# Indexer key, rope key and indexer weights in one half block, multiplied in float32, with rotary tables of half the width

## The chip, the cores and the metric

The kernel runs on one core of one Trainium2 chip, in one launch. The metric is device time in microseconds (us). The kernel before took 1176.38 us as the median of three runs (1176.0, 1177.55 and 1176.38 us). The engines are PE (TensorE, which multiplies matrices), DVE (VectorE), ACT (ScalarE), POOL (GpSimd) and SP (SyncE, which issues the transfers). Each runs its instructions in a fixed order and waits for the others by semaphores.

## The reference, cut to what matters

One decoder layer on 256 tokens of width 1024. A combined projection gives the inputs of two attention branches. Branch A selects 64 keys for each query by an indexer, and its rotary encoding covers all 64 dimensions of a head. Branch B is a latent attention with a rotary key of 32 dimensions. The gates merge the two, and 32 experts with a top-4 router follow.

```python
SPLITS = (A_WIDTH, A_WIDTH, A_WIDTH, IDX_HEADS * IDX_DIM, IDX_DIM, IDX_HEADS,
          Q_LORA, KV_LORA, QK_ROPE, 2 * D_MODEL)
def rope(x, positions):
    half = x.shape[-1] // 2
    inv_freq = ROPE_THETA ** (-jnp.arange(half, dtype=jnp.float32) / half)
    ...
    cos, sin = jnp.cos(ang).astype(x.dtype), jnp.sin(ang).astype(x.dtype)
    x1, x2 = x[..., :half], x[..., half:]
    return jnp.concatenate([x1 * cos - x2 * sin, x1 * sin + x2 * cos], axis=-1)
# the indexer of branch A, in a block of 128 queries
rel = jax.nn.relu(jnp.einsum('bthd,bsd->bths', qib, k_idx).astype(jnp.float32) * idx_scale)
score = jnp.einsum('bths,bth->bts', rel, wb.astype(jnp.float32) * w_scale)
...
_, sel = lax.top_k(score, k_sel)
```

Three of the narrow pieces of the projection matter here: the indexer key (`k_idx`, 64 columns), the indexer weights (`wb`, 8 columns) and the rope key (32 columns). Together they are 104 columns.

## The kernel before, in words

**The input projection.** The weights of the projection are packed on the host into blocks of 1 MB (`w_pre`), each of 128 partitions by 2048 numbers, and each block has two halves of 8 x 128 columns. A half gives 128 rows of a transposed result. The product is formed in three fp32r multiplications (L152 to L154): the weight is split into a high and a low part (`wh`, written by ACT at L143, and `wl`, the difference, written at L144 by DVE, or by POOL where the running number of the part stands in the list `POOL`), and the input likewise (`xh` at L148, `xl` at L149). So a half block is 24 matmuls of 256 columns: xh with wh, xl with wh, xh with wl for each of 8 slices. Up to three pairs of `wh` and `wl` are in use at a time.

**Block 0.** Its first half holds the indexer key twice (64 columns, repeated to fill 128), its second half the rope key twice and the indexer weights. Both halves land in one PSUM bank. `keys_first` copies the second result to SBUF (`kr_in`), and the two are rotated separately: `indexer_key` to `kim`, `rope_key` to `kr` and `kbm`.

**The rotary tables.** `rotary_tables` (L264 to L285) reduces the angles of two kinds of rotation on DVE, both side by side in tiles of 512 columns, and takes four sines of 256 columns on ACT. `tr_` serves branch A and the indexer, `trb` branch B. A rotation (`rope`, L204 to L208) is a shuffle of the source within groups of 32 partitions and a multiplication by the cosine on DVE, a multiplication by the signed sine on POOL, and an addition. The source may be a PSUM bank: the bank is free once the shuffle and the first multiplication have read it.

**PSUM.** The projection uses the tiles called `bank`, of which there are two. A third half block group can start on PE only after the readers of the first are done.

**What sets the order.** The list `ORDER` names the pieces of the head of the kernel in sequence (`k0` the keys, `tab` the tables, `ki` and `kr` the two rotations, `qi` the indexer queries, `lat` the latents, `ix` the indexer scores and so on). A scheduler then places the instructions of each engine by estimated durations, so that a change in one piece can move others. At L342 DVE forms the indexer scores, at L348 POOL masks them, at L352 and L353 DVE selects, eight at a time. At L375 DVE writes the low part of a latent, the last reader of that latent's bank.

**After the head.** From about 225 us the experts run, in pairs (L1021 and L1062 on PE). Their weights arrive as 1 MB transfers into a ring of slots. A slot is filled again as soon as PE has used it, and in the head the same ring carries the weights of the projection.

Of the kernel before, what the change touches and what calls it, by code (L numbers as in the profile page):

```python
# [52 lines left out]
POOL = "1 4 5 10 14 15 17 18 19 21 22 29 36 38 40 41 43"  # L53
# [4 lines left out]
def decoder_layer(ctx: ExitStack, tc: tile.TileContext, A, dbg=None):  # L58
# [59 lines left out]
    def load(i, k, n=2048):  # L118

        if i == 0:  # L120
            t = w0
        else:
            t = slot()
            sy.dma_start(t[:, :n], A["w_pre"][i][:, :n])
        return t[:, :n].rearrange("p (k c) -> p k c", k=k)
# [58 lines left out]
    for _ in range(20):  # L184
        te.matmul(idle[:, :P], ones, ones, start=True, stop=True)
# [54 lines left out]
    kr_in = work.tile([P, 1, T], F32, name="kr_in", tag="sq")  # L240
# [18 lines left out]
    def keys_first():
        for a in range(2):  # L260
            ps = half_proj(0, a)
        se.copy(kr_in, ps[:, 1:2])
        held["ki"] = ps

    def rotary_tables():
        pos = tmp1[:, 1]
        ve.tensor_copy(pos, pos_i)
        ang = tmp1[:, 2:4]
        ve.tensor_scalar(ang[:, 0], pos, cc[:, 0:1], None, op0=OP.mult)
        ve.tensor_scalar(ang[:, 1], pos, cc[:, 1:2], None, op0=OP.mult)  # L270
        rn = tmp2[:, 0:2]
# [4 lines left out]
        rc = tmp2[:, 2:4]  # L276
        ve.tensor_scalar(rn, ang, HALF_PI, -2 * math.pi, op0=OP.is_gt, op1=OP.mult)
        ve.scalar_tensor_tensor(rc, ang, HALF_PI, rn, op0=OP.add, op1=OP.add)

        for i, (src, j) in enumerate(((rc, 0), (ang, 0), (rc, 1), (ang, 1))):  # L280
            d = tr_[:, i] if i < 2 else trb[:, i - 2, 0]
            ve.tensor_scalar(d, src[:, j], PI_IN, -PI_IN, op0=OP.min, op1=OP.max)
            se.activation(d, d, AF.Sin)
            if i % 2:
                ve.tensor_scalar(d, d, cc[:, 2:3], None, op0=OP.mult)  # L285

    def indexer_key():
        rope(held["ki"][:, 0:1], 1, tab_a(1), [(kim, (slice(0, P), slice(0, 1)))])

    def rope_key():  # L290

        kr = work.tile([P, T], F32, name="kr", tag="sq")
        rope(kr_in, 1, [trb[:, i, 0:1] for i in range(2)],
             [(kr[:, None, :], (slice(0, P), slice(0, 1)))])
        for c in range(2):
            hs = slice(64 - 64 * c, 96 - 64 * c)
            se.copy(kbv[hs, :, c], kr[hs, None, :].to_broadcast([32, 4, T]))
        wiT = work.tile([64, T], F32, name="wiT", tag="sq")
# [298 lines left out]
    def router_tables():  # L597
# [6 lines left out]
        ge.tensor_scalar(lnv, lnv, cc[:96, 4:5], None, op0=OP.mult)  # L604
# [647 lines left out]
def _layout(inputs):  # L1252
# [13 lines left out]
    c[:, 0] = theta ** (-(p % 16 + 16 * (p // 32 % 2)).astype(np.float32) / np.float32(32))
    c[:, 1] = theta ** (-(p % 16).astype(np.float32) / np.float32(16))
    c[:, 2] = np.where(p % 32 < 16, -1.0, 1.0)
    c[:, 3] = p % 4 >= 2
    c[:, 4] = np.where(p // 8 % 4 == 1, np.float32(ALPHA), 1)  # L1270
# [17 lines left out]
```

## Time and profile before

| what | us |
|---|---|
| median of three runs | 1176.38 |
| the profiled execution | 1175.76 |
| its span, first to last instruction | 1174.1 |
| PE busy, over the span | 1089.6 (93%) |
| DVE busy | 333.3 (28%) |
| ACT busy | 221.8 (19%) |
| POOL busy | 136.3 (12%) |

The mean granted TensorE clock is 0.995 of full speed. The averages hide three stages. Up to about 225 us the projection, the attention and the router run, and all engines take part. From there to about 1105 us the experts run with the transfers at some 420 GB/s, and the last 69 us finish without new weights. The profiled execution is 0.62 us shorter than the median; the sums of this text are made against the profiled execution.

### The profile page before, as it was taken

To read this page: it belongs to the slowest core of one execution; us is meant where nothing else is said; L and a number is where in the kernel's file an instruction comes from. 1 tells how busy PE (TensorE), PEld (TensorE's weight loads), DVE (VectorE), ACT (ScalarE), POOL (GpSimd) and SP (SyncE) were. 2 spreads that over 40 slices of the span, in tenths; PEclk is the share of its full clock that TensorE was granted. 3 is DMA by queue.
4 is the path that set the end of the run, shared out by engine and by line. 5 is a ranking of instruction groups with operands and counts; after the bars stand their busy time and mean duration, and the time that the engine had idled before them with its cause. 6 is when DMAs were issued, how large, how long until landed. Compare 5 with 4: busy or idle time off the path is not lost.

```text
span 1174.1 us, 14174 instructions
## 1 busy us (share of the span) xinstructions
PE 1089.6 (93%) x5807; PEld 579.6 (49%) x5808; DVE 333.3 (28%) x702; ACT 221.8 (19%) x427; POOL 136.3 (12%) x127
## 2 busy tenths in 40 slices
PE   7999999999999999999999999999999999898985
PEld 7988889744343443434444444344444444343431
DVE  7887636713122111111111111111111111111113
ACT  4557734321011010101010101010101010101011
POOL 5574563200000100000001000000000000000001
PEclk9999999999999999999999999999999999999998
DMA  8433659799999999999999999999999999999993
GB/s 326 181 109 144 249 199 377 297 409 388 421 420 419 421 403 420 420 421 420 420 421 420 420 421 420 420 421 420 420 421 420 420 420 420 421 420 420 421 420 131
DMA packets 64239, 439.74 MB, mean 375 GB/s; under 512 B 8437, under 2 KB 8682, under 8 KB 11690
## 3 DMA queue, kind: packets, MB, share of 16 engines
q1 hardware_dynamic: 64170, 438.79, 91.3%
q8 instruction: 47, 0.77, 0.3%
q14 instruction: 22, 0.18, 0.0%
HBM read 437.71 MB, written 1.05 MB: 374 GB/s over the span
## 4 chain that ended last, share of the span: by engine, by line
DMA 55%; PE 28%; DVE 2%; ACT 1%; issue 0%; SPq 0%; DVEq 0%; ACTq 0%
DMA w<-w_up 36%; DMA w<-w_down 19%; PE pair L1021 13%; PE bank L1062 5%; PE misc L776 1%; PE pair L1062 1%; PE misc L977 1%; PE misc L154 1%; PE misc L152 1%; PE misc L153 1%; PE pair L152 1%; PE pair L154 1%; PE pair L153 1%; PE misc L910 0%; DMA braw<-b_down 0%; PE pair L790 0%
## 5 line engine op out<-in xcount | busy, mean ns | idle before, releaser
L1021 PE MATMUL pair<-w,xg 128*64 128x512 f32 x2032 | 490.0, 597 | 47.4 <-DMA w<-w_up 47.3
L1021 PEld LDWEIGHTS pair<-w,xg 128*64 128x64 f32 x2032 | 181.9, 136 | 314.7 <-issue 183.5
L1062 PE MATMUL bank<-w,y 128*64 128x512 f32 x960 | 213.2, 596 | 1.8
L1062 PEld LDWEIGHTS bank<-w,y 128*64 128x64 f32 x960 | 70.1, 137 | 127.5 <-issue 115.2
L889 DVE TENSOR_TENSOR acc<-acc,misc 128x512 f32<-128x512 f32 x60 | 38.7, 684 | 175.7 <-PE misc L977 175.6
L152 PE MATMUL bank<-xh,wh 128*128 128x256 f32 x256 | 73.9, 289 | 4.1 <-DVE rm L205 2.7
L899 DVE TENSOR_SCALAR y<-pair 128x512 f32<-128x512 f32 x32 | 22.0, 687 | 194.1 <-ACT y L892 194.1
L154 PE MATMUL bank<-xh,wl 128*128 128x256 f32 x256 | 72.9, 285 | 2.9 <-DVE wl L144 2.9
L153 PE MATMUL bank<-xl,wh 128*128 128x256 f32 x256 | 72.2, 282 | 1.3 <-DVE xl L149 1.3
L989 ACT CAST pgT<-bank 128x256 fp32r<-128x256 f32 x16 | 6.0, 373 | 340.3 <-PE bank L987 340.3
L776 PEld LDWEIGHTS misc<-pm,h 128*128 128x128 f32 x512 | 59.8, 192 | 13.3 <-issue 12.5
L178 POOL TENSOR_TENSOR rstd<-rstd,mhalf 128x1 f32<-128x1 f32 x4 | 2.6, 662 | 546.9 <-DVE rstd L684 546.9
L776 PE MATMUL misc<-pm,h 128*128 128x128 f32 x512 | 64.1, 278 | 0.0
L970 DVE SCALAR_TENSOR_TENSOR yp<-bank,gsl,yp 128x512 fp32r<-128x512 f32 x30 | 21.1, 745 | 148.2 <-ACT yp L968 148.2
L892 ACT ACTIVATE y<-pair 128x512 f32<-128x512 f32 x32 | 19.0, 597 | 192.8 <-PE pair L1021 192.8
L968 ACT ACTIVATE yp<-bank,gsl 128x512 fp32r<-128x512 f32 x30 | 19.0, 684 | 178.3 <-PE bank L1062 178.3
L152 PEld LDWEIGHTS bank<-xh,wh 128*128 128x128 f32 x256 | 48.8, 190 | 6.2 <-issue 3.0
L154 PEld LDWEIGHTS bank<-xh,wl 128*128 128x128 f32 x256 | 48.8, 191 | 4.0 <-DVE wl L144 3.8
L143 ACT CAST wh<-w 128x1024 fp32r<-128x1024 f32 (+1 forms) x42 | 42.7, 1024 | 41.9 <-PE bank L153 25.8
L153 PEld LDWEIGHTS bank<-xl,wh 128*128 128x128 f32 x256 | 48.9, 191 | 1.6 <-DVE xl L149 1.5
L768 DVE TENSOR_SCALAR xg<-misc,lnT 128x128 f32<-128x128 f32 x64 | 22.1, 404 | 92.5 <-PE misc L776 85.7
L144 DVE TENSOR_TENSOR wl<-w,wh 128x1024 fp32r<-128x1024 f32 (+1 forms) x26 | 40.4, 1554 | 16.1 <-ACT wh L143 16.1
(357 smaller groups left out, 1045.1 us busy)
## 6 DMA issues: line engine op xcount, KB each, us to landing
w<-w_up SPq DMA_DIRECT2D x254, 1024.0 KB, 19.8
w<-w_down SPq DMA_DIRECT2D x127, 1024.0 KB, 19.8
w<-w_pre SPq DMA_DIRECT2D x27, 1024.0 KB, 5.0
w<-w_pre SPq DMA_DIRECT2D x3, 512.0 KB, 7.3
w<-w_pre SPq DMA_DIRECT2D x2, 768.0 KB, 12.7
w<-xT SPq DMA_DIRECT2D x4, 256.0 KB, 6.4
xr<-x SPq DMA_DIRECT2D x2, 512.0 KB, 4.5
acc<-w_up SPq DMA_DIRECT2D x1, 1024.0 KB, 6.8
```

What stands on the lines that cost most here:

```text
L143: se.copy(hi, w[:, a])
L144: (ge if flip[0] in aside else ve).tensor_sub(lo, w[:, a], hi.bitcast(F32))
L152: te.matmul(out, lhs[0], rhs[0], start=start, stop=False)
L153: te.matmul(out, lhs[0], rhs[1], start=False, stop=False)
L154: te.matmul(out, lhs[1], rhs[0], start=False, stop=stop)
L768: ve.tensor_scalar(dst, src, lnT[:, k:k + 1], lnT[:, 8 + k:9 + k], op0=OP.mult, op1=OP.add)
L776: te.matmul(pt[:, k4], h[:, b, k * P:(k + 1) * P], pm[:, b].rearrange("p e s -> p (e s)"), start=(b == 0), stop=(b == NT - 1))
L889: ve.tensor_add(acc[:, b, half(c)], acc[:, b, half(c)], ps)
L899: ve.tensor_scalar(li, up[c][:, 1], LIMIT + 1.0, 1.0 - LIMIT, op0=OP.min, op1=OP.max)
L970: ve.scalar_tensor_tensor(y[:, 1, half(c)], dn[c], gs, y[:, 0, half(c)].bitcast(F32), op0=OP.mult, op1=OP.subtract)
L1021: te.matmul(up[c % 2][64 * i:64 * i + 64, c // 2], xg[k // 4][:, k % 4, 64 * i:64 * i + 64], ws[i][:, 512 * c:512 * c + 512], start=False, ...
L1062: te.matmul(dn[c][64 * i:64 * i + 64, :], aT[:, 2 * a + j, 64 * i:64 * i + 64], ws[i][:, D * j + 512 * c:D * j + 512 * c + 512], start=Fal ...
```

## The change

The 104 columns of indexer key, rope key and indexer weights now stand in one half block: key in rows 0 to 63, rope key in 64 to 95, weights in 96 to 103 of one result. It is multiplied in one pass of float32 (`mm8` on the unsplit input `xt` and weight), without `wh` and `wl`. Block 0 is loaded only in its first half. One rotation serves both keys, with a table (`tab`) of 256 columns a function in which rows 0 to 63 hold the angles of branch A and rows 64 to 127 those of branch B. ACT copies the halves of `tab` to where the wider tables were (`tr_`, `trb`), and copies the second half of `kim`. The constants shrink by a column, and the warm-up has 12 matmuls in place of 20. The list `POOL` is the same list of parts with all numbers two lower and without the first entry, because the two parts of block 0 are gone.

```diff
-POOL = "1 4 5 10 14 15 17 18 19 21 22 29 36 38 40 41 43"
+POOL = "2 3 8 12 13 15 16 17 19 20 27 34 36 38 39 41"
...
-    sy.dma_start(w0[:, D:], A["w_pre"][0][:, D:])
...
-    for _ in range(20):
+    for _ in range(12):
         te.matmul(idle[:, :P], ones, ones, start=True, stop=True)
...
     def keys_first():
-        for a in range(2):
-            ps = half_proj(0, a)
-        se.copy(kr_in, ps[:, 1:2])
-        held["ki"] = ps
+
+        ps = held["ki"] = bank()[:, None, :T]
+        w = w0[:, :D].rearrange("p (k c) -> p k c", k=KD)
+        mm8(ps[:, 0], lambda k: w[:, k], lambda k: xt[:, k])
...
-        for c in (C1, C2, C3):
+        for c in (C1, C2):
             ve.scalar_tensor_tensor(ang, rn, -c, ang, op0=OP.mult, op1=OP.add)
...
+        ve.scalar_tensor_tensor(tab[:, 1], rn, -C3, ang, op0=OP.mult, op1=OP.add)
+        ve.tensor_scalar(rn, tab[:, 1], HALF_PI, -2 * math.pi, op0=OP.is_gt, op1=OP.mult)
+        ve.scalar_tensor_tensor(tab[:, 0], tab[:, 1], HALF_PI, rn, op0=OP.add, op1=OP.add)
+
+        ve.tensor_scalar(tab, tab, PI_IN, -PI_IN, op0=OP.min, op1=OP.max)
+        se.activation(tab, tab, AF.Sin)
+        ve.tensor_scalar(tab[:, 1], tab[:, 1], cc[:, 1:2], None, op0=OP.mult)
 
     def indexer_key():
-        rope(held["ki"][:, 0:1], 1, tab_a(1), [(kim, (slice(0, P), slice(0, 1)))])
+        ps = held["ki"]
+        kr = held["kr"] = work.tile([P, 1, T], F32, name="kr", tag="sq")
+        rope(ps, 1, [tab[:, i, None] for i in range(2)],
+             [(kim[0:64], (slice(0, 64), slice(0, 1))), (kr[64:96], (slice(64, 96), slice(0, 1)))])
+        se.copy(kim[64:P], kim[0:64])
+        for c in range(2):
+            se.copy(tr_[64 * c:64 * c + 64], tab[0:64])
 
     def rope_key():
...
-        ve.tensor_scalar(wiT[32:40], kr_in[32:40, 0], 8 ** -0.5, None, op0=OP.mult)
+        se.activation(wiT[32:40], held["ki"][96:104, 0], AF.Copy, scale=8 ** -0.5)
...
-        ge.tensor_copy(trb[:, :, 1], trb[:, :, 0])
-        for i in range(2):
-            for c in range(2):
+        for c in range(2):
+            se.copy(trb[64 - 64 * c:P - 64 * c, :, c], tab[64:P])
+            for i in range(2):
                 ge.memset(trb[64 * c:64 * c + 64, i, c], 1.0 - i)
...
-    w8[:, :, 32:40] = wi[:, :, OWI:OWI + 8]
-    for i in (0, 64):
-        w8[:, :, i:i + ROPE] = wi[:, :, OKR:OKR + ROPE]
-    blocks = [flat(wi[:, :, 2 * [OKI + d for d in mixed]], w8)]
+    w8[:, :, :104] = wi[:, :, [OKI + d for d in mixed] + r(OKR, ROPE) + r(OWI, 8)]
+    blocks = [flat(w8)]
```

In the changed kernel the line numbers are lower: L143 and L144 become L139 and L140, L148 becomes L144, L152 to L154 become L148 to L150, L204 to L208 become L200 to L204, L342 becomes L334, L348 L340, L361 L353 and L375 L367.

First, ACT from its first cast on. Before, the table functions are the four at L283, and `kr_in` is the copy of the second key:

```order
L143 CAST wh<-w 128x1024 x3
L262 COPY kr_in<-bank 128x256
L143 CAST wh<-w 128x1024
L283 ACTIVATE tr__158<-tr__158 128x256
L283 ACTIVATE trb<-trb 128x256
L283 ACTIVATE tr__158<-tr__158 128x256
L143 CAST wh<-w 128x1024
L283 ACTIVATE trb<-trb 128x256
L143 CAST wh<-w 128x1024 x3
L297 COPY kbm<-kr 32x4x256 x2
```

The same place now, where L274 is the one sine, L284 and L298 the copies of its halves, and L289 takes the indexer weights out of the bank of the keys:

```order
L139 CAST wh<-w 128x1024 x3
L274 ACTIVATE tab<-tab 128x512
L284 COPY tr__149<-tab 64x512 x2
L298 COPY trb<-tab 64x2x256 x2
L139 CAST wh<-w 128x1024
L289 ACTIVATE wiT<-bank 8x256
L139 CAST wh<-w 128x1024
L291 COPY kbm<-kr 32x4x256 x2
L282 COPY kim<-kim 64x256
```

The last reader of the bank of the keys on ACT was the copy to `kr_in`, ahead of the tables; now it is L289, behind the sine, four copies and a cast.

Second, PE where the third latent (L152 on `bank_479` before, L148 on `bank_411` now) begins. Before, a whole latent on the bank `bank_407` stands ahead of it:

```order
L154 MATMUL bank_407<-xh_102,wl_409 128x256
L361 MATMUL misc_371<-ones_109,sq_403 128x1 x2
L226 MATMUL pair_682<-kim_153,rot_470 128x128
L152 MATMUL bank_479<-xh_102,wh_480 128x256
L153 MATMUL bank_479<-xl_103,wh_480 128x256
```

And now, with `bank_339` the second latent and `bank_272` the second pair of indexer queries, whose place in PSUM `bank_411` takes over:

```order
L150 MATMUL bank_339<-xh_101,wl_341 128x256
L150 MATMUL bank_272<-xh_101,wl_375 128x256
L148 MATMUL bank_272<-xh_101,wh_374 128x256
L149 MATMUL bank_272<-xl_102,wh_374 128x256
L150 MATMUL bank_272<-xh_101,wl_375 128x256
L148 MATMUL bank_272<-xh_101,wh_374 128x256
L149 MATMUL bank_272<-xl_102,wh_374 128x256
L150 MATMUL bank_272<-xh_101,wl_375 128x256
L353 MATMUL misc_303<-ones_108,sq_368 128x1 x2
L148 MATMUL bank_411<-xh_101,wh_412 128x256
```

The last seven matmuls of the indexer queries have moved behind the second latent, to just ahead of the third.

Third, POOL where the scores of the first 256 columns are masked. Before:

```order
L348 AFFINE_SELECT sc<-sc 128x128
L206 TENSOR_TENSOR rxs<-rxs,trb 128x512
L208 TENSOR_TENSOR rot<-rm,rxs 128x512
L348 AFFINE_SELECT sc<-sc 128x256
L144 TENSOR_TENSOR wl<-w,wh 128x1024 x2
L206 TENSOR_TENSOR rxs<-rxs,trb 128x512
```

And now:

```order
L340 AFFINE_SELECT sc<-sc 128x128
L202 TENSOR_TENSOR rxs<-rxs,trb 128x512
L204 TENSOR_TENSOR rot<-rm,rxs 128x512
L140 TENSOR_TENSOR wl<-w,wh 128x1024
L340 AFFINE_SELECT sc<-sc 128x256
L140 TENSOR_TENSOR wl<-w,wh 128x1024
```

One of the two low parts has moved ahead of the mask of 256 columns.

## Rows read from the trace of the kernel before

**Rows 1.** Page, part 2: GB/s moved in each of the 40 slices.

```profile
GB/s 326 181 109 144 249 199 377 297 409 388 421 420 419 421 403 420 420 421 420 420 421 420 420 421 420 420 421 420 420 421 420 420 420 420 421 420 420 421 420 131
```

**Rows 2.** Windows: span, busy of PE, PEld, DVE, ACT, POOL, clock, DMA share, GB/s.

```profile
25.00:50.00 25.00, 24.92 (x195) 23.44 (x196) 19.60 (x39) 14.17 (x21) 13.32 (x14) 0.93 0.57 225
50.00:60.00 10.00, 8.99 (x74) 8.63 (x74) 9.72 (x30) 4.23 (x7) 8.35 (x6) 1.00 0.32 116
205.00:220.00 15.00, 15.00 (x99) 13.63 (x98) 11.47 (x14) 6.62 (x9) 2.76 (x3) 1.00 0.62 226
463.00:1105.00 642.00, 593.37 (x2786) 267.08 (x2782) 106.27 (x214) 59.59 (x121) 4.73 (x6) 1.00 1.01 420
```

**Rows 3.** Chain of work that ended last: start, duration, what.

```profile
235.22 1.90 PE misc L776 x16
...
463.35 19.83 DMA w<-w_down
```

**Rows 4.** Timeline, SP 0 to 12: start, duration, engine, line, operation.

```profile
3.17 0.43 SPq L106 DMA_DIRECT2D w<-w_pre  x1
...
8.57 3.70 SPq L124 DMA_DIRECT2D w<-w_pre  x6
```

**Rows 5.** Timeline, 13 to 25 us, DVE, ACT and POOL; brackets: idle before, releaser.

```profile
13.78 1.42 DVE L275 SCALAR_TENSOR_TENSOR tmp<-tmp,tmp 128x512 f32<-128x512 f32 x2
14.39 2.00 ACT L143 CAST wh<-w 128x1024 fp32r<-128x1024 f32 x2 [2.82 <-DMA w<-w_pre]
15.47 1.23 DVE L144 TENSOR_TENSOR wl<-w,wh 128x1024 fp32r<-128x1024 f32 x1 [0.28 <-ACT wh L143]
16.46 5.37 POOL L144 TENSOR_TENSOR wl<-w,wh 128x1024 fp32r<-128x1024 f32 x2 [8.16 <-ACT wh L143]
16.61 2.92 DVE L275 SCALAR_TENSOR_TENSOR tmp<-tmp,tmp 128x512 f32<-128x512 f32 x1
19.80 2.31 DVE L277 TENSOR_SCALAR tmp<-tmp 128x512 f32<-128x512 f32 x1
24.33 0.42 DVE L205 TENSOR_TENSOR rm<-bank,tr__158 128x256 f32<-128x256 f32 x1 [0.28 <-ACT tr__158 L283]
```

**Rows 6.** Timeline, PE, 19 to 29 us.

```profile
19.80 0.28 PE L153 MATMUL bank<-xl,wh 128*128 128x256 f32 x1
...
21.96 0.28 PE L154 MATMUL bank<-xh,wl 128*128 128x256 f32 x1
24.90 0.45 PE L152 MATMUL bank<-xh,wh 128*128 128x256 f32 x1 [2.67 <-DVE rm L205]
...
28.14 0.41 PE L152 MATMUL bank<-xh,wh 128*128 128x256 f32 x1
```

**Rows 7.** Groups by form, 0 to 60 us: busy us, mean ns, idle before.

```profile
L148 ACT CAST xh<-w 128x512 fp32r<-128x512 f32 x4 | 2.5, 618 | 1.6 <-DMA w<-xT 1.6
...
L297 ACT COPY kbm<-kr 32x1024 f32<-32x1024 f32 x2 | 2.1, 1044 | 1.9 <-POOL kr L208 1.9
...
L204 DVE STREAM_SHUFFLE rxs<-bank 128x512 f32<-128x512 f32 x4 | 2.9, 736 | 0.0
...
L205 DVE TENSOR_TENSOR rm<-bank,tr__158 128x512 f32<-128x512 f32 x2 | 1.4, 675 | 0.0
```

**Rows 8.** Timeline, 50 to 60 us, POOL, DVE and PE.

```profile
53.76 0.47 DVE L342 SCALAR_TENSOR_TENSOR sc<-rel,wi,sc 128x256 f32<-128x256 f32 x1
54.30 0.40 POOL L348 TENSOR_SCALAR_AFFINE_SELECT sc<-sc 128x256 f32<-128x256 f32 x1 [1.29 <-DVE sc L342]
54.41 0.50 PE L361 MATMUL misc<-ones,sq 128*128 128x1 f32 x4
54.67 4.79 POOL L144 TENSOR_TENSOR wl<-w,wh 128x1024 fp32r<-128x1024 f32 x2
55.13 0.47 DVE L375 SCALAR_TENSOR_TENSOR cq<-bank,vecT,cq 128x256 fp32r<-128x256 f32 x1
55.66 0.39 PE L152 MATMUL bank<-cq,wh 128*128 128x256 f32 x1 [0.75 <-DVE cq L375]
```

More of the change, by code (lines that the diff above doesn't have):

```diff
@@ L118, in load @@
     def load(i, k, n=2048):
[L120 to L124, printed above, removed]
+        t = slot()
+        sy.dma_start(t[:, :n], A["w_pre"][i][:, :n])
         return t[:, :n].rearrange("p (k c) -> p k c", k=k)
@@ L239, in decoder_layer @@
     trb = att.tile([P, 2, 2, T], F32, name="trb", tag="p1")
-    kr_in = work.tile([P, 1, T], F32, name="kr_in", tag="sq")
     wi = soon.tile([P, NT, 8], F32, name="wi")
@@ L259, in keys_first @@
     def keys_first():
-        for a in range(2):
-            ps = half_proj(0, a)
-        se.copy(kr_in, ps[:, 1:2])
-        held["ki"] = ps
+        ps = held["ki"] = bank()[:, None, :T]
+        w = w0[:, :D].rearrange("p (k c) -> p k c", k=KD)
+        mm8(ps[:, 0], lambda k: w[:, k], lambda k: xt[:, k])
     def rotary_tables():
-        pos = tmp1[:, 1]
+        pos, rn, ang = tmp1[:, 1], tmp1[:, 2], tmp1[:, 3]
         ve.tensor_copy(pos, pos_i)
-        ang = tmp1[:, 2:4]
-        ve.tensor_scalar(ang[:, 0], pos, cc[:, 0:1], None, op0=OP.mult)
@@ L270, in rotary_tables @@
-        ve.tensor_scalar(ang[:, 1], pos, cc[:, 1:2], None, op0=OP.mult)
-        rn = tmp2[:, 0:2]
+        ve.tensor_scalar(ang, pos, cc[:, 0:1], None, op0=OP.mult)
         ve.tensor_scalar(rn, ang, 1.0 / (2 * math.pi), MAGIC, op0=OP.mult, op1=OP.add)
         ve.tensor_scalar(rn, rn, MAGIC, None, op0=OP.subtract)
-        for c in (C1, C2, C3):
+        for c in (C1, C2):
             ve.scalar_tensor_tensor(ang, rn, -c, ang, op0=OP.mult, op1=OP.add)
-        rc = tmp2[:, 2:4]
-        ve.tensor_scalar(rn, ang, HALF_PI, -2 * math.pi, op0=OP.is_gt, op1=OP.mult)
@@ L278, in rotary_tables @@
[L278 to L285, printed above, removed]
-    def indexer_key():
-        rope(held["ki"][:, 0:1], 1, tab_a(1), [(kim, (slice(0, P), slice(0, 1)))])
+        ve.scalar_tensor_tensor(tab[:, 1], rn, -C3, ang, op0=OP.mult, op1=OP.add)
@@ L290, in rope_key @@
     def rope_key():
-        kr = work.tile([P, T], F32, name="kr", tag="sq")
-        rope(kr_in, 1, [trb[:, i, 0:1] for i in range(2)],
-             [(kr[:, None, :], (slice(0, P), slice(0, 1)))])
+        kr = held["kr"]
+        wiT = work.tile([64, T], F32, name="wiT", tag="sq")
+        se.activation(wiT[32:40], held["ki"][96:104, 0], AF.Copy, scale=8 ** -0.5)
         for c in range(2):
-            hs = slice(64 - 64 * c, 96 - 64 * c)
-            se.copy(kbv[hs, :, c], kr[hs, None, :].to_broadcast([32, 4, T]))
@@ L298, in rope_key @@
-        wiT = work.tile([64, T], F32, name="wiT", tag="sq")
-        ve.tensor_scalar(wiT[32:40], kr_in[32:40, 0], 8 ** -0.5, None, op0=OP.mult)
+            se.copy(kbv[64 - 64 * c:96 - 64 * c, :, c], kr[64:96].to_broadcast([32, 4, T]))
         pt = misc()
@@ L568, in bias_parts @@
         if name == "up":
-            ge.tensor_scalar(raw, raw, cc[:96, 3:4], None, op0=OP.add)
+            ge.tensor_scalar(raw, raw, cc[:96, 2:3], None, op0=OP.add)
         three_parts(raw, out)
@@ L602, in router_tables @@
         ve.tensor_copy(lnT, pt[:, :32])
-        ge.tensor_scalar(lnv, lnv, cc[:96, 4:5], None, op0=OP.mult)
+        ge.tensor_scalar(lnv, lnv, cc[:96, 3:4], None, op0=OP.mult)
         three_parts(lnv, lnp)
@@ L1262, in _layout @@
     arrays["xT"] = np.ascontiguousarray(arrays["x"].T.reshape(KD, P, T).transpose(1, 0, 2))
-    c = np.zeros((P, 5), np.float32)
+    c = np.zeros((P, 4), np.float32)
     p = np.arange(P)
     theta = np.float32(10000.0)
[L1266 to L1270, printed above, removed]
+    c[:64, 0] = (theta ** (-(p % 16 + 16 * (p // 32 % 2)).astype(np.float32) / np.float32(32)))[:64]
+    c[64:, 0] = (theta ** (-(p % 16).astype(np.float32) / np.float32(16)))[64:]
+    c[:, 1] = np.where(p % 32 < 16, -1.0, 1.0)
+    c[:, 2] = p % 4 >= 2
+    c[:, 3] = np.where(p // 8 % 4 == 1, np.float32(ALPHA), 1)
     arrays["consts"] = c
```

4 lines of the change are left out of this document (2 added, 2 removed).

## The prediction, made before the changed kernel had run

> **What bounds the kernel now.** I read the slices of the page first. The transfers move 109 to 409 GB/s in the first ten slices of 29 us and about 420 from the eleventh to the last but one [rows 1]. The windows say the same by stage: from 463 to 1105 us the DMA engines are busy all the time at 420 GB/s, with PE at 593 of 642 us [rows 2]. The chain that ended last is transfer after transfer there [rows 3]. None of that is touched by the change. Yet the head is not hidden behind it: from 205 to 220 us PE is busy in 15.00 of 15 us while DMA is at 0.62 [rows 2], because a transfer needs a slot that PE has emptied. So the stream begins when PE lets it, and a microsecond that PE loses or gains anywhere in the head moves the end by a microsecond.
>
> In the head I looked for the places where PE stops. From 25 to 50 us it is busy in 24.92 of 25 us [rows 2]. Before that there is one large stop: it ends at 24.90 after 2.67 us, with DVE's `rm` at L205 as releaser [rows 6]. That is the first multiplication of the indexer key's rotation, which frees the keys' bank. `rm` waited for the sine [rows 5], the sine for the table work on DVE, and DVE had stood twice: L275 took 2.92 us at 16.61 where two earlier ones took 1.42 together (0.71 each), and L277 took 2.31 us at 19.80 [rows 5]. Both times POOL was writing two `wl`, in 5.37 us from 16.46 to 21.83 [rows 5]. After the stop PE runs at half clock (1.2 of 2.4 GHz): 15 matmuls from 24.90 to 28.14 are 0.216 us each, 19 before it from 19.80 to 21.96 are 0.114 [rows 6]. That is 16 times 0.1 = 1.6 us.
>
> **The Trainium skill on this.** The rows show DVE with two SBUF operands held until POOL's `wl` was through [rows 5]. The page "SBUF — State Buffer", section "Who interferes with whom", gives the cause: a DVE instruction with two SBUF inputs, or in a two-port mode, shares a port pair with GpSimd, and the one that comes second stands until the other's whole instruction is done. It speaks against this change, as halving the width of the table operations would by that rule not shorten the two waits; without it the 256-column operations would take about half of 0.71 us each, PE would resume about 2 us earlier, and the sum below would be about 2 us lower. Twice the rows show the wait, so the sum goes by it.
>
> **PE's own work.** Block 0 loses its 48 fp32r matmuls, 48 x 0.114 = 5.5 us [rows 6], and gains eight in float32. The nearest float32 row is the experts' gather: 16 records of 128x128 in 1.90 us [rows 3], each float32 matmul shown as two records, so 0.24 us for 128 columns and 0.475 for 256, 3.8 us in all. The saving is 1.7 us, bounds 0 to 5.5. I count it as nothing: PE then has its result at about 10.3 us, waits for block 1, ends block 1's two halves at about 20.9 us (before 22.2), and stops at the same place, the keys' bank. The eight missing warm-up matmuls lie ahead of the input's arrival and cost nothing for the same reason.
>
> **Loads.** The 0.5 MB of block 0's second half, issued at 3.17 [rows 4], goes. At 326 GB/s [rows 1] that is 1.6 us. Block 1's cast stood at 14.39, on its transfer [rows 5], which was issued at 8.57 [rows 4]. I put it at about 13.0, so the first `wl` is ready at 15.3 instead of 16.70 [rows 5]. Everything below hangs on that start.
>
> **The tables and the keys' bank (T1).** The three casts take 1.0 us each (2.00 for two) [rows 5], so POOL begins its two `wl` at about 15.1 and ends at 20.5. DVE's L271, with two SBUF inputs, comes at 15.3 and stands to about 18.0; the clamp L273 behind it stands to 20.5, as L277 did. The sine of 512 columns on ACT I put at 0.65 us (0.62 for ACT's cast of 512 [rows 7]): 21.2. The sign product brings 21.6. Now comes what the change adds: ACT has four copies of 64x512 and a cast ahead of L289, which reads the indexer weights out of the keys' bank. Four copies are 2.2 us by the casts' 0.62 each, with their starts a little closer than that, at most 4 x 1.04 = 4.2 by the copies of 1024 columns [rows 7]; the cast is 1.0, L289 0.3. That gives 25.1. PE resumes at 25.1 instead of 24.90: T1 = +0.2. Bounds: -2.0 where the clamp gets in between POOL's two operations (20.5 becomes 18.4), +2.1 with the copies at 1.04. The clock falls as before, since the stop is longer (4.2 us against 2.67).
>
> **The third latent (T2).** The last seven matmuls of the indexer queries now come right ahead of the third latent, which takes over their bank. It can start when their rotation's shuffle (0.736) and multiplication (0.675) have read it [rows 7], 1.41 us, less 0.25 for two of the four matmuls with one column in between (0.50 for four [rows 8]): T2 = +1.2. Before, a whole latent of 24 matmuls, 2.7 us, stood between and covered it, and PE did not stop in that stretch [rows 2]. Bounds: 0 where DVE is early, because PE was held elsewhere first, to 2.4, where a `wl` of 1.23 us [rows 5] stands ahead of the rotation on DVE.
>
> **The mask on POOL (T3).** POOL's `wl` of 1024 now starts ahead of the mask of 256 columns. Before, POOL idled 1.29 us until DVE's last score product, 0.47 us at 53.76, had released the mask; the two `wl` followed in 4.79 us from 54.67, and L375 came at 55.13, unhindered [rows 8]. Now that score product, with two SBUF inputs, meets a running `wl` and waits up to its end, 4.79 / 2 = 2.4 us; behind it on DVE stands the latent's low part (now L367), for which PE was already waiting at 55.66 [rows 8]. DVE is busy in 9.72 of these 10 us [rows 2], so nothing absorbs it. T3 = +2.4, bounds 0 (the score product comes first) to 4.8 (both `wl` hold DVE).
>
> **The clock again (T4).** PE then stands for 0.75 + 2.4, about 3.2 us, longer than the stop of 2.67 behind which the clock halved. I add 1.6 us at even chance: T4 = +0.8, bounds 0 to 1.6.
>
> **The rest.** The numbers of the parts have shifted, so some later parts use other buffers, and the last gates and the merge stand in another order on PE, ACT and DVE. I have no row that prices it: 0, with 2 us to either side, about the price of one such stop [rows 6]. What DVE and POOL are spared (the tables' and rotation's instructions, and the 1024-column `wl` of block 0) lies where PE is full or waits for something else, so it brings nothing.
>
> The sum is 0.2 + 1.2 + 2.4 + 0.8 = +4.6 us: 1175.76 + 4.6 = 1180.4 against the profiled execution, and 1181.0 against the median, which is 0.62 above it. I give the latter.
>
> **The rivals.** *A, faster:* the clamp slips in between POOL's two `wl`. At 18.0, when L271 ends, POOL's second is only waiting or just begun; against it speaks that in the trace the two POOL operations took 5.37 us, only 0.6 over the undisturbed 4.79 [rows 5, 8], so POOL seized the second at once. Then PE resumes 2.0 us sooner after a stop of only about 2.0 us, between the 0.75 that left the clock alone and the 2.67 that didn't: -2.0 - 1.6, with T2 +1.2 and T3 at 0, is -2.4, 1174.0. *B, no change:* T3 does not come about, because DVE reaches the score product before POOL reaches its `wl`; T1 and T2 alone are +1.4, 1177.8. For it speaks that the scheduler placed the `wl` where it saw POOL idle; against it, that POOL idled only 1.29 us there and `wl` takes 2.4. *C, slower still:* the copies cost 1.04 each (+1.9) and both clock falls come whole (+0.8): +7.3, 1183.7. That block 0 is shorter without the saving reaching the end is part of all of these; that it does reach the end (-1.7 alone, from PE's work) would need the table chain to end before 20.9 us, which no row supports.
>
> **How the numbers follow.** The forecast has 0.46, A 0.14, B 0.22, C 0.18. Less than 0.2% (2.35 us) to either side, 1174.03 to 1178.73, is about what a measurement of this kernel can't tell from no change. A is just faster and takes 0.14; B is no change, with 0.22; the forecast, from 1178.8 to 1183.2 by the terms' bounds around it, and C are slower: 0.64. The range reaches from 1174.4, which leaves out most of A, to 1184.6, past C, where further losses of the reordered tail lie.
>
> **What would show it.** Right: one PE stop of about 4 us that ends near 25 us with ACT's read of the indexer weights as releaser; DVE's clamp stretched to over 2 us; a PE stop of about 1 us ahead of the third latent; a score product of 2 to 3 us on DVE near 54 us with PE waiting behind it; the experts starting 4 to 5 us later. Wrong: PE resuming before 23.5 us, a first stop that leaves the clock whole, or a score product of 0.47 us; any of them takes away the term in question, and two together the forecast.

## The result, and the profile after

The changed kernel took 1183.63 us as the median of five runs (1181.16 to 1184.67), the kernel before 1177.02 us (1176.0 to 1178.28). The ratio is 1.0059, with a 95% interval of 1.0047 to 1.0072: 6.6 us slower. It was run a second time, unaltered, beside three of the experiments and took 1183.6 us against 1176.44, a ratio of 1.0069 (1.0054 to 1.0085). Two slow executions, one of 2171.33 us among e9's and one of 3778.17 us of the kernel before, are left out of every time and ratio here. The profiled execution took 1183.63 us with a span of 1181.8, so its span is 7.7 us longer than the one of the kernel before.

I looked first at where PE stops in the head. These are rows of its timeline in the changed kernel (start, duration, engine, line, operation; in brackets the idle time ahead and what ended it):

```profile
13.42 0.58 PE L148 MATMUL bank<-xh,wh 128*128 128x256 f32 x1 [3.52 <-ACT wh L139]
24.86 0.29 PE L294 MATMUL misc<-ident,wiT 8*128 8x8 f32 x2 [2.47 <-ACT wiT L289]
40.61 0.61 PE L353 MATMUL misc<-ones,sq 128*128 128x1 f32 x4 [0.27 <-ACT sq L364]
41.94 0.36 PE L148 MATMUL bank<-xh,wh 128*128 128x256 f32 x1 [0.72 <-DVE rm L201]
58.25 0.39 PE L148 MATMUL bank<-cq,wh 128*128 128x256 f32 x1 [2.70 <-DVE cq L367]
```

The second row answers to the stop of [rows 6]. PE resumes at 24.86 instead of 24.90, and what releases it is now ACT's read of the indexer weights. The fourth row is the third latent, and the last is the place of [rows 8], where the stop was 0.75 us and is now 2.70. The four stretches of [rows 2], in windows (span, busy of PE, PEld, DVE, ACT and POOL, granted clock, DMA share, GB/s):

```profile
25.00:50.00 25.00, 23.84 (x190) 22.47 (x190) 16.20 (x31) 13.81 (x20) 9.32 (x6) 0.93 0.50 171
50.00:60.00 10.00, 7.30 (x63) 7.22 (x62) 9.79 (x23) 3.76 (x7) 8.43 (x5) 1.00 0.45 170
205.00:220.00 15.00, 15.00 (x107) 13.94 (x106) 12.86 (x15) 6.37 (x8) 6.44 (x6) 1.00 0.45 158
463.00:1105.00 642.00, 592.78 (x2788) 265.67 (x2785) 106.58 (x216) 58.21 (x119) 4.72 (x6) 1.00 1.01 420
```

PE is busy 24.92 - 23.84 = 1.08 us less from 25 to 50 and 8.99 - 7.30 = 1.69 less from 50 to 60. Such differences can't be added up, since the same window holds other work in the two kernels. What can be compared are marks: places in the order of PE that have the same projection matmuls ahead of them in both kernels, less the 48 of block 0. The first mark, the sums of squares of a latent, stands at 54.41 in the kernel before [rows 8] and at 55.05 in the changed one. The next two are the first products with `kbm` and with `kam`, each first in the kernel before, then in the changed one:

```profile
55.05 0.50 PE L353 MATMUL misc<-ones,sq 128*128 128x1 f32 x4
```

```profile
66.85 2.23 PE L226 MATMUL pair<-kbm,rot 128*128 128x256 f32 x12 [0.83 <-DVE kbm L421]
69.49 2.23 PE L222 MATMUL pair<-kbm,rot 128*128 128x256 f32 x12 [0.87 <-DVE kbm L413]
```

```profile
105.80 1.57 PE L226 MATMUL pair<-kam,rot 64*128 64x128 f32 x14
108.72 1.57 PE L222 MATMUL pair<-kam,rot 64*128 64x128 f32 x14
```

The last mark is the experts' first gather in the chain of waits, at 240.40 instead of 235.22 [rows 3]. So the changed kernel is 0.64 us late at 55 us, 2.64 at 69, 2.92 at 109 and 5.18 where the experts start: 2.3 us are lost behind 109 us. The second profile of the changed kernel has the four marks at 54.34, 69.52, 108.47 and 240.26.

```profile
240.40 1.90 PE misc L768 x16
```

From there the stream of weights carries the loss to the end, with 420 GB/s in both kernels from 463 to 1105 us. The last transfer of the chain ends at 1111.16 instead of 1105.07 us, 6.1 us later, so another 0.9 us have come on the way, between 421 and 469 us, where the chain passes from PE to the transfers. The remaining 1.6 us of the span lie in the last stage. After a PE stop of 1.98 us, which both kernels have, the last expert's 16 matmuls took 3.44 us in the kernel before and 4.88 in the changed one, at a lower clock (1.00 from 1140 to 1154 us before, 0.88 from 1146 to 1160 now). The changed kernel's second profile, with a span of 1180.3 us, shows 3.44 again. In order, the kernel before, the changed one, and the changed one again:

```profile
1143.34 3.44 PE pair L1062 x16
```

```profile
1149.66 4.88 PE pair L1054 x16
```

```profile
1149.56 3.44 PE pair L1054 x16
```

So this part comes and goes between executions of one kernel. I do not count it to the change, but no experiment settles it: the other ten profiles, e1 to e4 and e6 to e11, all show 4.39 to 5.81 us at this place.

### The profile page after: what moved, and what is told of

Same layout as the page of the kernel before. It is cut to its first block, busy times and chain, and to the rows that moved or that the text cites. A ratio compares the mean times of both kernels' runs of the same rounds, so it can differ in the third digit from the quotient of the medians.

```text
span 1181.8 us, 14065 instructions
## 1 busy us (share of the span) xinstructions
PE 1090.2 (92%) x5759; PEld 577.8 (49%) x5760; DVE 326.9 (28%) x693; ACT 221.8 (19%) x427; POOL 133.1 (11%) x123
## 4 chain that ended last, share of the span: by engine, by line
DMA 57%; PE 33%; DVE 5%; ACT 3%; issue 1%; POOL 0%; SPq 0%; DVEq 0%; ACTq 0%; POOLq 0%
DMA w<-w_up 37%; DMA w<-w_down 18%; PE pair L1013 12%; PE bank L1054 5%; PE bank L148 2%; PE bank L150 2%; PE bank L149 2%; PE misc L768 1%; PE pair L1054 1%; DVE wl L140 1%; ACT wh L139 1%; PE misc L969 1%; PE pair L148 1%; PE misc L148 1%; PE pair L150 1%
## 5 line engine op out<-in xcount | busy, mean ns | idle before, releaser
L148 PE MATMUL bank<-xh,wh 128*128 128x256 f32 x240 | 70.6, 295 | 4.8 <-ACT wh L139 3.5
L150 PE MATMUL bank<-xh,wl 128*128 128x256 f32 x240 | 69.6, 291 | 2.2 <-DVE wl L140 2.2
L149 PE MATMUL bank<-xl,wh 128*128 128x256 f32 x240 | 68.8, 287 | 0.0
L148 PEld LDWEIGHTS bank<-xh,wh 128*128 128x128 f32 x240 | 46.9, 195 | 6.2 <-ACT wh L139 4.6
L139 ACT CAST wh<-w 128x1024 fp32r<-128x1024 f32 (+1 forms) x40 | 40.7, 1024 | 43.5 <-PE bank L149 33.2
L150 PEld LDWEIGHTS bank<-xh,wl 128*128 128x128 f32 x240 | 46.8, 195 | 3.4 <-DVE wl L140 2.9
L565 POOL CAST bup<-braw 96x512 bf16<-96x512 f32 x4 | 4.3, 1068 | 347.0 <-PE pair L782 346.9
```

Of the source, the lines that this page charges most:

```text
L139: se.copy(hi, w[:, a])
L148: te.matmul(out, lhs[0], rhs[0], start=start, stop=False)
L149: te.matmul(out, lhs[0], rhs[1], start=False, stop=False)
L150: te.matmul(out, lhs[1], rhs[0], start=False, stop=stop)
```

## The experiments

Ten more kernels ran, and the changed one a second time (e5). "e1" and so on are the names of the runs, and a ratio is to the kernel before on the same chip.

**e1: the buffers of the late parts.** In the changed kernel block 0 no longer counts as two parts. Two parts fewer shift which spare buffers the late weights use. The experiment gives the numbers back:

```diff
-    flip, spare, aside = [0], [], [int(i) for i in POOL.split()]
+    flip, spare, aside = [2], [], [int(i) + 2 for i in POOL.split()]
```

> The changed kernel with its parts counted from 2 instead of 0 (and the list POOL two higher), so that each late part of the weights uses the spare buffer it used in the kernel before; the head up to 130 us is in the same order as in the changed kernel. Theory 1 (the stops of PE between 178 and 193 us, 1.07 + 0.43 + 0.75 = 2.25 us, come from the other buffers): they go, the experts start about 2.8 us after the kernel before instead of 5.2, and the time is about 1181.3. Theory 2 (they come from weights that land later because the head is late): they stay, and the time stays at 1183.6.

Measured: 1178.97 us, ratio 1.0026 (1.0012 to 1.0040), against 1.0059 and 1.0069 for the changed kernel. PE's waits from 165 to 200 us (line, what for, us in total, times, longest), first of the changed kernel, then of e1:

```profile
PE misc L148 <- ACT sy L139: 1.5, 2, 1.1
PE pair L148 <- ACT mh L144: 0.8, 1, 0.8
PE bank L148 <- ACT gT L496: 0.6, 1, 0.6
PE bank L150 <- DVE wl L140: 0.3, 1, 0.3
```

```profile
PE bank L150 <- DVE wl L140: 0.3, 1, 0.3
```

The waits for ACT, 2.9 us, are gone, and the experts start at 236.89 instead of 240.40, 3.5 us earlier. Where the first block lands doesn't explain it: its cast stood at 11.53 in e1, at 12.32 in the changed kernel and at 11.66 in its second profile, whose experts start at 240.26. Nor does the head: the mark of `kam` stands at 108.69 in e1 and at 108.72 in the changed kernel. So theory 1 is shown, and the gain is larger than forecast: the numbers of the late parts are worth 3.4 to 3.5 us, all of it behind 109 us. With the numbers the order on PE behind 130 us also changes in places (the third group of matmuls on `pT` and `va` starts at 155.12 in e1 and at 157.18 in the changed kernel). Buffers and order are not told apart.

**e2: the indexer weights read early.** ACT's read of the keys' bank moves from behind the sine, copies and a cast to right behind the keys' product:

```diff
         mm8(ps[:, 0], lambda k: w[:, k], lambda k: xt[:, k])
+        wiT = held["wiT"] = work.tile([64, T], F32, name="wiT", tag="sq")
+        se.activation(wiT[32:40], ps[96:104, 0], AF.Copy, scale=8 ** -0.5)
```

> The changed kernel with one instruction moved: ACT reads the indexer weights out of the keys' bank right after the keys are multiplied, ahead of the casts, instead of behind the sine, four copies and a cast. Theory 1 (the bank is what PE waits for, and that read is its last reader): PE resumes at about 21.2 instead of 24.86, released by DVE's first multiplication of the rotation, the stop is under 0.5 us instead of 2.47, the clock stays whole there (1.6 us), and the experts start 3.6 to 5.2 us earlier: 1178.4 to 1180.0. Theory 2 (PE's stop is only one of several waits in a row; the next half block's weights or the tables hold it anyway): the gain is under 1.5 us, 1182 to 1183.6.

Measured: 1180.65 us, ratio 1.0031 (1.0019 to 1.0044). PE's stops in e2:

```profile
14.46 0.58 PE L148 MATMUL bank<-xh,wh 128*128 128x256 f32 x1 [3.50 <-ACT wh L139]
28.07 0.35 PE L148 MATMUL bank<-xh,wh 128*128 128x256 f32 x1 [1.74 <-DVE rm L201]
```

The stop at the keys' bank is gone altogether: PE goes on from 15.72 through the third half block to 26.33. So the bank was what held it, and that read its last reader. But the forecast of a stop under 0.5 us failed. Behind it the next bank is not free, that of the first queries, whose rotation on DVE stands behind a `wl` that waits for ACT's copies and cast. PE reaches the sums of squares at 53.63 instead of 55.05, 1.4 us earlier, but the product with `kbm` at 68.67 instead of 69.49, and the experts start at 239.59 instead of 240.40: 0.8 us, where 3.6 or more was forecast. The time lies between the ranges of the two theories.

**e3: no low part on POOL at the start.**

```diff
-POOL = "2 3 8 12 13 15 16 17 19 20 27 34 36 38 39 41"
+POOL = "8 12 13 15 16 17 19 20 27 34 36 38 39 41"
```

> The changed kernel with the parts 2 and 3 taken out of the list POOL, so that DVE writes those two low parts itself (1.23 us each) and POOL does none of it before 25 us. Theory 1 (POOL's two operations hold DVE's L271 and L273 for 2.2 us each): L271 takes 0.42 us instead of 2.63 and L273 0.43 instead of 2.52, DVE gets back about 4.3 us and spends 2.5, the tables are ready about 2 us earlier and PE resumes at 22.3 to 23.0 instead of 24.86; the time is 2 to 3.5 us lower, 1180 to 1181.6. Theory 2 (these two operations are long of themselves, by operand or place): they stay at about 2.5 us each, the two more low parts come on top, and the time is 2 us higher.

Measured: 1182.98 us, ratio 1.0047 (1.0032 to 1.0063). The two operations on DVE and POOL's two in the changed kernel:

```profile
14.39 5.05 POOL L140 TENSOR_TENSOR wl<-w,wh 128x1024 fp32r<-128x1024 f32 x2 [8.26 <-ACT wh L139]
14.54 2.63 DVE L271 SCALAR_TENSOR_TENSOR tab<-tab,tmp 128x256 f32<-128x256 f32 x1
17.21 2.52 DVE L273 TENSOR_SCALAR tab<-tab 128x512 f32<-128x512 f32 x1
```

and in e3:

```profile
15.82 0.42 DVE L271 SCALAR_TENSOR_TENSOR tab<-tab,tmp 128x256 f32<-128x256 f32 x1
17.29 0.42 DVE L273 TENSOR_SCALAR tab<-tab 128x512 f32<-128x512 f32 x1
24.59 0.36 PE L148 MATMUL bank<-xh,wh 128*128 128x256 f32 x1 [1.73 <-DVE rm L201]
```

2.63 and 2.52 us become 0.42 each with POOL out of the way. The hold is shown, for an operation of 256 columns as much as for one of 512 [rows 5]. The Trainium skill's page "SBUF — State Buffer", section "Who interferes with whom", says the same: a DVE instruction with two SBUF inputs, beside a GpSimd instruction that reads SBUF, or one in a two-port mode, waits out the whole GpSimd instruction if that was issued first. The trace agrees, by 2.63 against 0.42 us. The gain in time is not shown: PE resumes at 24.59, held by the next rotation on DVE. The first cast stood at 13.60 there, 1.3 us later than in the changed kernel, and the intervals of the two kernels overlap.

**e4 and e6: the low part ahead of the mask.** e4 takes that part from POOL to DVE; e6 is e1 with another part on POOL in its stead:

```diff
-POOL = "2 3 8 12 13 15 16 17 19 20 27 34 36 38 39 41"
+POOL = "2 3 8 13 15 16 17 19 20 27 34 36 38 39 41"
...
-POOL = "2 3 8 12 13 15 16 17 19 20 27 34 36 38 39 41"
+POOL = "2 3 8 11 13 15 16 17 19 20 27 34 36 38 39 41"
```

> The changed kernel with part 12 taken out of the list POOL: the low part that stood ahead of the mask of 256 columns on POOL is written by DVE, behind the last score product. Theory 1 (that low part on POOL holds the score product, 2.40 us, and with it the latent's low part for which PE stands 2.70 us until 58.25): the score product takes 0.47 us, PE's stop shrinks to 1.2 to 1.7 us (DVE's own low part of 1.23 us takes some of it back). Later parts move too (buffers, gates), so the time is less certain: 1181 to 1184. Theory 2 (PE's stop there has another cause, such as the projection's weights): the stop stays at 2.5 us or more.

> The kernel of e1_rotation with part 11 in place of 12 in the list POOL: as many low parts on POOL, but ahead of the mask of 256 columns stands no low part of 1024 columns any more; the rest of the order up to 48 us is that of e1. Theory 1 (that low part holds the last score product and so the latent's low part for which PE stands 2.70 us): the product takes 0.5 to 0.9 us instead of 2.40, PE's stop near 57 us shrinks to under 1.5 us, and the time is 1 to 2 us under that of e1, 1177 to 1178. Theory 2 (the stop comes from the latent or its weights): it stays at 2.5 us or more and the time at 1179.

Measured: e4 1183.71 us, ratio 1.0053 (1.0035 to 1.0070); e6 1179.36 us, ratio 1.0029 (1.0015 to 1.0043). In the changed kernel the place reads, on POOL and DVE:

```profile
53.84 3.10 POOL L140 TENSOR_TENSOR wl<-w,wh 128x1024 fp32r<-128x1024 f32 x1
54.82 2.40 DVE L334 SCALAR_TENSOR_TENSOR sc<-rel,wi,sc 128x256 f32<-128x256 f32 x1
57.73 0.47 DVE L367 SCALAR_TENSOR_TENSOR cq<-bank,vecT,cq 128x256 fp32r<-128x256 f32 x1
```

In e4 the same product, the low part now on DVE, and PE's two stops:

```profile
53.42 0.46 DVE L334 SCALAR_TENSOR_TENSOR sc<-rel,wi,sc 128x256 f32<-128x256 f32 x1
54.07 1.36 DVE L140 TENSOR_TENSOR wl<-w,wh 128x1024 fp32r<-128x1024 f32 x1
56.07 0.39 PE L148 MATMUL bank<-cq,wh 128*128 128x256 f32 x1 [1.92 <-DVE cq L367]
64.23 0.70 PE L387 MATMUL misc<-dg,ones 128*128 128x256 f32 x2 [2.49 <-DVE dg L383]
```

and in e6 PE's two stops:

```profile
57.06 0.39 PE L148 MATMUL bank<-cq,wh 128*128 128x256 f32 x1 [1.94 <-DVE cq L367]
65.22 0.70 PE L387 MATMUL misc<-dg,ones 128*128 128x256 f32 x2 [2.50 <-DVE dg L383]
```

The product takes 0.46 us in e4, without the low part on POOL, so the hold is shown. In e6 it takes 1.32 us, with a multiplication of the rotation on POOL (L202, 1.49 us) beside it, more than the 0.9 forecast. PE's stop shrinks to 1.9 us only, with the low part now on DVE between the product and the latent's. And a stop of 2.5 us appears at 64 us, where the changed kernel has 1.5 and e1 has 1.2. Neither kernel is faster than what it is to be compared with. The experts start at 242.46 in e4 (240.40 in the changed kernel) and at 237.06 in e6 (236.89 in e1). DVE is full here (9.79 of 10 us in the windows above); that what is moved to it comes back later for this reason is not shown. For e6, theory 1 has the stop (under 1.5 us) and the time wrong too.

**e5** is the changed kernel again (above).

> The changed kernel again, unaltered, on the same chip as the next three, so that they are compared with it and not with a run of another hour. It should take 6 to 7 us more than the kernel before (1183 to 1184), with PE's stops at 24.9, 41.9, 58.3 and 182 to 193 us in the same places; the cast of block 1 may stand up to 1 us elsewhere, as its transfer lands.

**e7: all of these together.** The edits of e1, e2 and e6, and the copies of the branch A table on DVE:

```diff
-            se.copy(tr_[64 * c:64 * c + 64], tab[0:64])
+            ve.tensor_copy(tr_[64 * c:64 * c + 64], tab[0:64])
```

> e1 and e6 together, the early read of the indexer weights of e2, and the two copies of the branch A table on DVE instead of ACT (two operations of 64x512 behind the rotation's first product), so that the rotation of the first queries does not stand behind ACT's copies. Theory 1 (the loss is the sum of the stops named: the keys' bank and the next one behind it, the third latent, the mask, the buffers): PE's stops near 25, 41 and 57 us are each under 1 us, the experts start 1 to 3 us earlier than in the kernel before, and the time is 1173 to 1176, a little under the kernel before. Theory 2 (stops taken away at one place come back at the next): not under 1177.

Measured: 1175.87 us, ratio 1.0000 (0.9986 to 1.0013). The experts start at 233.45, 1.8 us ahead of the kernel before, with stops of 0.42 us at 53.81 and 1.49 at 60.97 and none at the third latent. One large stop is left, for the bank of the first queries:

```profile
28.39 0.36 PE L148 MATMUL bank<-xh,wh 128*128 128x256 f32 x1 [2.08 <-DVE rm L201]
```

The loss of the change is undone, and theory 1 holds with that exception. The 1.8 us by which the experts start earlier don't show in the time: the last transfer still ends 1.7 us ahead of the kernel before, and then the last stage's 16 matmuls take 5.81 us instead of 3.44.

**e8: PE kept busy ahead of block 1.** e1 with matmuls on constants behind the keys' product:

```diff
         mm8(ps[:, 0], lambda k: w[:, k], lambda k: xt[:, k])
+        for _ in range(14):
+            te.matmul(idle[:, :P], ones, ones, start=True, stop=True)
```

> The kernel of e1_rotation with 14 float32 matmuls of 128 columns on constants (no part of the result) behind the keys' product, so that PE does not stand from 10 us until the first query block's weights come, and the clock should not fall there. Theory 1 (PE waits for the keys' bank anyway, so its speed before 22 us counts for nothing, as the prediction has it): block 1 runs at full clock and ends 2 to 3 us earlier, PE resumes within 0.3 us of where it does in e1, and the time is that of e1 within 1 us, 1178 to 1180. Theory 2 (the idle time that the saved matmuls leave costs by the clock): 1.6 us or more under e1, 1177.4 or less.

Measured: 1179.76 us, ratio 1.0029 (1.0018 to 1.0039), as e1. From 14 to 20 us, first e1 and then e8:

```profile
14.00:20.00 6.00, 6.00 (x40) 6.00 (x40) 5.26 (x4) 1.68 (x2) 4.67 (x2) 0.75 1.02 425
```

```profile
14.00:20.00 6.00, 5.48 (x46) 5.29 (x46) 4.96 (x6) 2.33 (x5) 5.67 (x3) 1.00 1.01 422
23.40 0.29 PE L296 MATMUL misc<-ident,wiT 8*128 8x8 f32 x2 [3.53 <-ACT wiT L291]
```

The clock stays whole (46 matmuls instead of 40 in the 6 us), the stop grows to 3.53 us, and the time is the same. PE resumes at 23.40 instead of 24.08 in e1, more than the 0.3 us allowed (one table operation of DVE came ahead of POOL's first `wl` here and took 0.43 us); at 69 us nothing of it is left (`kbm` at 69.45, in e1 at 69.46). PE's speed before 22 us counts for nothing here.

**e9 and e11: the queries ahead of the latents.** e9 is e1, and e11 the kernel before, each with

```diff
-k0 tab ki qi00 qi01 kr qi10 lat0 lat1 qi11 lat2 uq00 lat3 ix00 lat4 ix10 norms uq01 ix01 causal kn kb0 vb0
+k0 tab ki qi00 qi01 kr qi10 qi11 lat0 lat1 lat2 uq00 lat3 ix00 lat4 ix10 norms uq01 ix01 causal kn kb0 vb0
```

> The kernel of e1_rotation with the second half of the second indexer queries (qi11) ahead of the first two latents in ORDER, as PE had it in the kernel before. The scheduler also places the low parts and score products of 40 to 60 us otherwise. Theory 1 (PE's stop at the third latent, 0.72 and 0.27 us, comes from the bank of the queries that end right ahead of it): no stop of PE between 30 and 45 us, and 1 us gained at 45 us beside e1; the time 1 us under e1 or, where the later stops grow, no different: 1177 to 1179. Theory 2 (it comes from the weights' low part or from the latent): a stop of 0.7 us or more stays between 35 and 45 us.

> The kernel before, unaltered but for ORDER, with qi11 ahead of the latents as in e9. Theory 1 (the place of the queries matters only where they end right ahead of a latent that takes their bank, which is not so in the kernel before): no change within 0.2%, 1174.5 to 1178.5. Theory 2 (that order is better for either kernel, so that e10's gain is none of the change's): 2.4 us or more under the kernel before, 1174 or less.

Measured: e9 1183.75 us, ratio 1.0049 (1.0033 to 1.0066); e11 1180.33 us, ratio 1.0027 (1.0016 to 1.0038). In e9 PE stands nowhere from 25 to 50 us, but at 82 us:

```profile
25.00:50.00 25.00, 25.00 (x206) 23.40 (x205) 18.86 (x29) 14.03 (x22) 11.42 (x7) 1.00 0.52 197
82.34 0.58 PE L148 MATMUL bank<-xh,wh 128*128 128x256 f32 x1 [3.63 <-ACT wh L139]
```

The stop at the third latent is that of the bank, as theory 1 had it. A stop of 3.63 us came with the new order, the experts start at 240.36 instead of 236.89 in e1, and theory 1's forecast of the time failed. The kernel before gets 3 us slower by the same edit, which neither theory expected. Its experts start at 234.88, 0.3 us earlier, and in its last stage the 16 matmuls take 5.13 us instead of 3.44. But the execution profiled was the fastest of its seven (1177.11 us, median 1180.33), so the profile leaves most of the 3 us open. Theory 2 is refuted: this order alone is no gift to either kernel.

**e10: what the experiments point to.** e7 with the queries first and e8's matmuls.

> e7_together with the queries first as in e9, and 14 matmuls of 128 columns on constants (no part of the result) around the keys' product, which keep PE from standing. Theory 1 (with each stop removed at its own place, what is left of the change is its saving): the first queries' two blocks and the keys run at full clock, no stop over 1.5 us before 60 us, the experts start 4 to 6 us earlier than in the kernel before, and the time is 1171 to 1173.5. Theory 2 (the head cannot gain on the kernel before, since POOL and DVE bound it behind 60 us): 1175 or more, as e7.

Measured: 1170.98 us (1169.56 to 1172.17), ratio 0.9950 (0.9937 to 0.9963): 5.9 us faster than the kernel before and some 13 faster than the changed one. The experts start 5.2 us before those of the kernel before. PE's larger stops in the first 60 us, and the start of the experts in the chain:

```profile
12.92 0.39 PE L148 MATMUL bank<-xh,wh 128*128 128x256 f32 x1 [0.41 <-ACT wh L139]
14.27 0.29 PE L297 MATMUL misc<-ident,wiT 8*128 8x8 f32 x2 [0.84 <-ACT wiT L262]
26.64 0.39 PE L150 MATMUL bank<-xh,wl 128*128 128x256 f32 x1 [0.73 <-DVE wl L140]
58.10 0.70 PE L390 MATMUL misc<-dg,ones 128*128 128x256 f32 x2 [2.19 <-DVE dg L386]
229.98 1.90 PE misc L771 x16
```

Here the idle time that the shorter block 0 leaves is filled, no bank holds PE before 50 us, and the 5.2 us are still there when the last transfer ends (1099.69 instead of 1105.07). That this gain is the saving of the change is argued, not shown: of e10's edits only the order was tried on the kernel before (e11), not the matmuls on constants, the table copies on DVE or the other part on POOL. One stop of 2.19 us at 58 us is longer than theory 1 allowed.

## Why the prediction was right, and where it was not

**Right: slower, through the head.** 4.6 us were forecast and 6.6 measured, inside the range. The stream has the same rate in both profiles, and the 5.2 us by which the experts start later are still there at 1105 us. In the ten profiles of e1 to e4 and e6 to e11 the shift at the experts' start and the shift at the end of the last transfer agree within 0.4 us.

**"Anywhere in the head" was too wide.** A microsecond gained early did not reach the end. The changed kernel, its second profile, e1 and e8, which have the same projection matmuls ahead of these marks, reach the sums of squares at 55.05, 54.34, 54.11 and 53.57 us, but all four reach the product with `kbm` at 69.45 to 69.52. In between PE waits for DVE, which is busy in 9.79 of 10 us from 50 to 60 in the changed kernel, and in the three where PE came earlier its clock fell behind the stop of 2.7 us. With up to 1.5 us less of T1 and T2 the mark at 69 us stands the same.

**PE's own work, right.** The keys' product is 16 records in 3.71 us, 0.46 us for 256 columns, where 3.8 were worked out from the experts' gather:

```profile
6.02 3.71 PE L154 MATMUL bank<-w 128*128 128x256 f32 x16
```

That PE's speed there is worth nothing e8 shows from the other side.

**Loads and T1, right for the reason given.** Block 1's cast stood at 12.32 instead of 14.39 (forecast 13.0). The two holds were 2.63 and 2.52 us, and the rest of the chain on ACT was

```profile
12.32 1.99 ACT L139 CAST wh<-w 128x1024 fp32r<-128x1024 f32 x2 [3.33 <-DMA w<-w_pre]
19.77 0.63 ACT L274 ACTIVATE tab<-tab 128x512 f32<-128x512 f32 x1 [3.84 <-DVE tab L273]
20.82 1.25 ACT L284 COPY tr__149<-tab 64x512 f32<-64x512 f32 x2 [0.42 <-DVE tab L275]
22.10 1.24 ACT L298 COPY trb<-tab 64x512 f32<-64x512 f32 x2
24.43 0.38 ACT L289 ACTIVATE wiT<-bank 8x256 f32<-8x256 f32 x1
```

with copies of 0.62 us each, where I had 2.2 for the four and they took 2.5. PE resumed at 24.86, forecast 25.1: T1 is -0.04 instead of +0.2 (PE resumed at 24.20 in the second profile). The stop was 2.47 us and not about 4, because PE ended block 1 at 22.39 and not at 20.9: after its stop of 3.52 us it had run 18 matmuls from 15.06 to 18.90 at 0.213 us each, half clock, which the prediction had not seen. The clock fell after the stop as forecast, for 15 matmuls from 26.18 to 29.39. Rival A did not come about: POOL's second `wl` took its turn before the clamp, as in the kernel before.

**T2, right in kind, too large.** The stop for the bank of the queries was 0.72 us, 1.2 forecast, and e9 takes it away by the order alone. The 1.08 us in the windows also hold 0.27 us for ACT's `sq` just ahead of it and 0.17 for POOL's `rot` at 45.91. T1 and T2 together are the 0.64 us at the first mark, 1.4 forecast.

**T3, right in kind, too large.** The score product stood for 2.40 us as forecast, but PE's stop grew from 0.75 to 2.70, by 1.95 instead of 2.4. That is what separates the first two marks, 0.64 and 2.64 us late.

**T4, the chance fair, the price too large.** In the first profile the clock was whole from 50 to 60 us although PE stood 2.70 us, about as long as the 2.67 us behind which it fell in the kernel before [rows 6]. In the second profile of the same kernel it fell behind the same stop of 2.70 us (e5, windows as above):

```profile
58.00:60.00 2.00, 2.00 (x14) 2.00 (x13) 1.83 (x10) 0.00 (x0) 1.34 (x1) 0.61 0.11 41
60.00:62.00 2.00, 2.00 (x11) 2.00 (x11) 1.33 (x5) 0.83 (x1) 0.02 (x1) 0.53 0.71 217
```

It also fell in e1, e2, e3 and e8, behind 2.68 to 2.70 us. The length of a stop alone does not tell. And the fall cost nothing: PE's next stop, for ACT's `vb`, ends at 65.77 us with it and at 65.73 without, so T4 was 0 where 0.8 was forecast.

**The rest, wrong: this is the step that failed.** "I have no row that prices it: 0, with 2 us to either side" should have been about +2.5: from 2.64 us late at 69 us to 5.18 at the experts' start, 2.3 of it behind 109 us. The shifted numbers of the parts put late weights into other buffers, and PE then stood for ACT from 174 to 193 us; e1 shows that it is the numbers. The forecast came out near the truth by luck: the four terms ahead of it were 2.0 us too high together (2.6 measured, 4.6 forecast) while this was 2.5 too low. What is left, 0.9 us between the start and the end of the stream and 1.6 in the last stage, was in no term. The second profile shows the latter to come and go; it has 1.1 us of the former, e2 and e3 with the same numbers have none, and what it is made of I have not settled.

**The rivals.** B had T3 absent, which the trace refutes. C needed copies of 1.04 us, which took 0.62, and both falls of the clock, of which the second came only in the second profile and cost nothing; it came nearest in time, 1183.7, by none of its reasons.

## What to carry to other kernels

Half the work of a stage that waits for something else is worth nothing, so look for what that stage waits for first: here the last reader of a PSUM bank, which the change itself had moved behind four copies. Where a list or a counter assigns engines and buffers by number, a part less at the start moves assignments far away; keep the numbers as they were, and test the change before anything else with them kept. Compare two orders by marks that have the same work ahead of them, and follow a gain from mark to mark: here up to 1.5 us gained by 55 us were gone at 69. A change that loses may still be the better base: with its large stops before 50 us taken away at their own places, and PE kept busy at the start, this one is 0.5% ahead of the kernel before, though not all of these edits were tried on that kernel.

## What the runs showed of the hardware that was not expected

A stop of 2.7 us was followed by half clock at 24.90 us in the kernel before, and at 58.25 us the changed kernel shows the whole clock in one execution (1.00) and at the same place, 57.54 us, about half in another (0.61 and 0.53). In the last stage one kernel shows 3.44 and 4.88 us for the same 16 matmuls behind the same stop. Of two `wl` in a row on POOL each held one operation of DVE: 2.63 and 2.52 us in the changed kernel (0.42 each in e3, without them), 2.92 and 2.31 in the kernel before. By these times the first held operation went when POOL's first was through, and the next one met POOL's second. In e8, where one operation of DVE came ahead of POOL (0.43 us), the next two took 2.31 and 1.73. The first block's transfer lands up to 2 us earlier or later between kernels that issue their transfers in the same order: its cast stood at 11.53 us in e1 and at 13.60 in e3, and at 12.32 and 11.66 in two executions of the changed kernel.
